# One decoder-layer step on one core: recurrent sample states in four partition quarters, and the first norm from token rows

## The chip, the cores and the metric

The kernel runs on one core of a Trainium2 chip. The time is device microseconds (us) of that core for one execution. The engines are TensorE (PE; PEld is its weight load), VectorE (DVE), ScalarE (ACT), GpSimd (POOL) and SyncE (SP), which issues nearly all transfers. Each engine runs its own instructions in the order in which they were written and waits on semaphores for the others.

## What is computed

One layer of a hybrid decoder, in float32, for a prompt of 512 tokens and a sample group of 8 sequences with 4 tokens each. All 544 tokens share the weights; the model width is 1024.

```python
x = x + 0.5 * swiglu_1(rmsnorm(x))            # 1024 -> 2816 -> 1024
z = rmsnorm(x) @ w_in                         # q,k,v of 8 attention heads; q,k,v,o and gates of 4 mLSTM heads
x = x + concat(attention, mlstm) @ w_out
x = x + 0.5 * swiglu_2(rmsnorm(x))
# mLSTM, one head, one sequence, T tokens, state C (128 x 128), n (128), m:
num = A @ v + w_inter * (q @ C)               # A: gated causal q.k within the chunk
den = rowsum(A) + w_inter * (q @ n)
h   = num / max(|den|, exp(-m_t))
C   = w_c * C + (w_s * k)^T @ v               # n likewise; w_c, w_s from the gates
```

The attention is a dilated causal window with three dilations. For the sample group it reads a cache of 2048 earlier positions per sequence. For the mLSTM each of the 8 sample sequences brings its own state of 4 heads, which is read once and written once. Prompt states start at zero.

## The kernel before

Activations lie transposed: model width on the 128 partitions, tokens along the free dimension (512 prompt columns S, then 32 sample columns). `x` is eight such tiles of 128 x 544.

**Products.** Each weight block and each activation tile is split into a high and a low half (`whi`, `wlo`; `xh`, `xl`), and three products high*high, high*low, low*high are summed in PSUM. A product covers 272 columns, so one 128-row step of one output block is six matmuls (`mm<-xh,whi` and so on, recorded at L283, where the helper `mm` stands). ScalarE makes `whi`, VectorE makes `wlo`. Two PSUM tiles `mm` take the products; four tiles `aux` serve all else: transposes (helper `tr`, L288), attention, mLSTM, norms. All calls of the other engines go through one wrapper, so all have line 224 and are told apart by their tiles.

**Stages.** Feed-forward 1 (a first plain part of four column blocks, then blocks in a fast form with seven products in place of eight, `oh`/`ol`), the input projection `w_in` with the attention and the mLSTM worked in between its products, the output projection `w_out`, feed-forward 2. The first pass of `w_out` multiplies the outputs of the first three mLSTM heads (`mixed[4..6]`, operands `mh`/`ml`), the second pass head four and the attention.

**Order.** While the program is built, a class `Order` keeps a clock for each engine from a small cost table. Everything beside the products is a generator ("thread") that says when its inputs will be ready and how many `aux` tiles it needs; between two steps of the products, `poll` lets those threads write whose time has come, by priority. What results is one fixed order for each engine. Nothing is reordered at run time.

**The start.** Transfers bring the four token blocks `xt` of the left model half, the sample rows `xst`, the first weight block, the right half, the second weight block, then the "up" weights. `start` (L821) transposes eight groups of four blocks and one of sample rows; each group is copied out, scaled into `xh` and `xl`, and squared (`sq`: six on POOL, two on ScalarE). The squares are added up (three on POOL, four on VectorE), a matmul with `onesd` sums over partitions, and the norm's factor `rb` follows in passes over 272 columns. The products take x without that factor; the rescale `zg = mm * rb` applies it.

**The mLSTM for the sample group** (`ml_k`, `ml_v`, `ml_head`, L1393 to L1610). The 32 sample tokens lie on partitions 0 to 31. Two tiles `C0`, each with four sequences' states of 128 x 129 (the last column is n), are read by one matmul for the part within the chunk (`aTs`, `vs`) and eight for the states, all adding to the same 32 rows; `qm` holds the scaled queries, masked once for each sequence. Then POOL spreads the values by sequence (`vb`) and scales the states by `w_c`; four matmuls of 32 rows (`kws`, `vb`), two sequences each, make the additions, and VectorE adds them to the states, which go out by a transfer. The head's output `hN` (prompt) and `hS` (sample) is normed, transposed, gated (`hf`) and split for `w_out`.

## Time and profile before

| | |
|---|---|
| median of 3 runs | 1160.46 us (1159.03 to 1163.38) |
| the profiled execution | 1159.89 us, its span 1158.1 us |
| busy in the span | PE 97%, PEld 92%, DVE 68%, ACT 44%, POOL 16% |
| products on TensorE | 7680, of 272 columns each |
| mean rate of transfers | 124 GB/s |

The stages by the trace: transposes and the first products to about 40 us, feed-forward 1 to about 403 us, `w_in` with attention and mLSTM to about 690 us, `w_out` to about 777 us, feed-forward 2 to the end. In a row of the timeline or of the groups, "128*32" behind a matmul is the part of the array that it uses (rows * columns), "128x129" the moving operand, "x16" the count of records, and "[2.54 <-ACT hS]" idle time before it and what ended it. Matmuls overlap, so the time that one takes from the engine is read from the start of the next.

### The profile page before, as it was taken

The page shows a single profiled execution, that of the slowest core. Times are in us where ns is not written, and L with a number is a line of the kernel's source. Part 1 is how long each engine was busy: PE and PEld are TensorE (multiplying, and loading weights), DVE is VectorE, ACT ScalarE, POOL GpSimd, SP SyncE. Part 2 cuts the span into 40 slices and gives each one's busy share as a digit, 9 for nine tenths or more (in the row PEclk, how much of TensorE's full clock was granted, in tenths as well). Part 3 has the DMA queues.
Part 4 walks back from the last instruction along what each step waited for, and adds up shares of the span by engine and source line. Part 5 has one row for each costly group of instructions (what it writes and reads, how often), then busy time and mean ns, then how long its engine had stood idle before and what let it go on. Part 6 is the DMA issues. An engine that isn't in the chain of part 4 may idle for free.

```text
span 1158.1 us, 21205 instructions
## 1 busy us (share of the span) xinstructions
PE 1127.3 (97%) x8722; PEld 1068.9 (92%) x8722; DVE 790.9 (68%) x1169; ACT 512.9 (44%) x913; POOL 189.5 (16%) x165
## 2 busy tenths in 40 slices
PE   6999999999999998999999998999999999999998
PEld 5999999999999998988977785999999999999998
DVE  5798337873586789889785455679883488627851
ACT  4455215551345456546542444354551255414541
POOL 4210000000000046487554022001100000000000
PEclk9999999999999999999999997999999999999999
DMA  7213412432134264766797641433142142422232
GB/s 220 79 38 118 138 39 74 145 111 93 35 120 134 88 208 109 214 208 190 235 311 247 210 162 30 138 110 110 35 149 74 38 143 76 146 74 74 64 102 59
DMA packets 140620, 143.20 MB, mean 124 GB/s; under 512 B 8068, under 2 KB 119204, under 8 KB 140524
## 3 DMA queue, kind: packets, MB, share of 16 engines
q1 hardware_dynamic: 140460, 141.84, 39.3%
q8 instruction: 69, 1.13, 0.4%
q14 instruction: 27, 0.22, 0.1%
q0 software_dynamic: 64, 0.00, 0.0%
HBM read 130.44 MB, written 9.15 MB: 121 GB/s over the span
## 4 chain that ended last, share of the span: by engine, by line
PE 82%; DVE 10%; ACT 3%; issue 2%; DMA 2%; SPq 0%; POOL 0%; ACTq 0%; DVEq 0%
PE mm L283 67%; PE aux L283 13%; PE aux L288 3%; DVE wlo L224 2%; ACT whi L224 1%; DMA kv<-in_cache_k_win_dram 1%; DVE rs L224 1%; DVE ws L224 1%; DVE dn L224 1%; DVE wraw L224 1%; DMA xt<-in_x_prompt_dram 0%; DVE bcum L224 0%; DVE xl L224 0%; DVE mo L224 0%; DVE cb L224 0%
## 5 line engine op out<-in xcount | busy, mean ns | idle before, releaser
L224 ACT CAST whi<-wraw 128x1024 fp32r<-128x1024 f32 (+3 forms) x180 | 173.9, 987 | 139.9 <-PE mm L283 115.4
L224 DVE TENSOR_TENSOR wlo<-wraw,whi 128x1024 fp32r<-128x1024 f32 (+3 forms) x180 | 211.7, 1185 | 19.8 <-ACT whi L224 19.6
L283 PE MATMUL mm<-oh,wlo 128*128 128x272 f32 x720 | 209.4, 291 | 2.9 <-DVE wlo L224 2.9
L283 PE MATMUL mm<-oh,whi 128*128 128x272 f32 x720 | 207.4, 288 | 0.0
L283 PE MATMUL mm<-ol,whi 128*128 128x272 f32 x720 | 207.2, 288 | 0.0
L283 PE MATMUL mm<-xh,whi 128*128 128x272 f32 x720 | 160.1, 304 | 0.8 <-DVE zg L224 0.7
L283 PE MATMUL mm<-xh,wlo 128*128 128x272 f32 x720 | 150.1, 290 | 2.9 <-DVE wlo L224 2.9
L283 PE MATMUL mm<-xl,whi 128*128 128x272 f32 x720 | 150.4, 291 | 0.0
L283 PE MATMUL mm<-hh,whi 128*128 128x272 f32 x704 | 146.2, 289 | 0.0
L283 PE MATMUL mm<-hl,whi 128*128 128x272 f32 x704 | 145.6, 288 | 0.0
L283 PE MATMUL mm<-hh,wlo 128*128 128x272 f32 x704 | 145.6, 288 | 0.0
L224 DVE SCALAR_TENSOR_TENSOR x<-mm,x 128x544 f32<-128x544 f32 x48 | 34.8, 725 | 157.9 <-PE mm L283 157.9
L283 PEld LDWEIGHTS mm<-oh,wlo 128*128 128x128 f32 x720 | 135.4, 188 | 6.0 <-DVE wlo L224 4.7
L283 PEld LDWEIGHTS mm<-ol,whi 128*128 128x128 f32 x720 | 135.6, 188 | 0.0
L283 PEld LDWEIGHTS mm<-oh,whi 128*128 128x128 f32 x720 | 135.5, 188 | 0.0
L283 PEld LDWEIGHTS mm<-xh,whi 128*128 128x128 f32 x720 | 114.1, 191 | 13.8 <-issue 10.7
L283 PEld LDWEIGHTS mm<-xh,wlo 128*128 128x128 f32 x720 | 114.4, 191 | 3.3 <-DVE wlo L224 3.3
L283 PEld LDWEIGHTS mm<-xl,whi 128*128 128x128 f32 x720 | 114.4, 191 | 0.0
L283 PEld LDWEIGHTS mm<-hl,whi 128*128 128x128 f32 x704 | 110.4, 188 | 0.0
L283 PEld LDWEIGHTS mm<-hh,whi 128*128 128x128 f32 x704 | 110.3, 188 | 0.1
L283 PEld LDWEIGHTS mm<-hh,wlo 128*128 128x128 f32 x704 | 110.4, 188 | 0.0
L224 ACT CAST whi<-ws 128x1024 fp32r<-128x1024 f32 x54 | 56.7, 1051 | 99.7 <-DVE ws L224 99.7
(295 smaller groups left out, 1930.9 us busy)
## 6 DMA issues: line engine op xcount, KB each, us to landing
wraw<-in_ffn_w_gate_dram SPq DMA_DIRECT2D x38, 512.0 KB
wraw<-in_ffn_w_up_dram SPq DMA_DIRECT2D x36, 512.0 KB
wraw<-in_ffn_w_down_dram SPq DMA_DIRECT2D x16, 1024.0 KB
kv<-in_cache_k_win_dram SPq DMA_DIRECT2D x56, 256.0 KB
kv<-in_cache_v_win_dram SPq DMA_DIRECT2D x56, 256.0 KB
wraw<-in_w_in_dram SPq DMA_DIRECT2D x16, 512.0 KB
wraw<-in_ffn_w_down_dram SPq DMA_DIRECT2D x8, 768.0 KB
wraw<-in_w_in_dram SPq DMA_DIRECT2D x6, 1024.0 KB
```

What stands on the lines that cost most here:

```text
L224: r = fn(*args, **kw)
L283: nc.tensor.matmul(out, lhsT, rhs, start=start, stop=stop, **kw)
L288: nc.tensor.transpose(out, in_, idn)
```

## The change

It has two parts.

**Sample states in four quarters.** A helper `four` issues the same matmul four times, to output partitions 0, 32, 64 and 96, in four column quarters of the array. With it the sample rows of keys and values, and of the gate columns, are transposed into all four quarters, so `kws`, `vs` and `hS` have 128 partitions. Quarter g stands for sequences 2g and 2g+1. The states are read by twelve matmuls: four for the part within the chunk, and twice four in which quarter g reads its own sequence; `qm` holds two masks in place of eight. Each state update is a matmul on the 32 rows of one quarter for two sequences (`vb` has the two sequences side by side, made by two ScalarE copies with a 0/1 column `bm4`); two such matmuls, on different rows of the array and into different `aux` tiles, are issued together, and VectorE scales and adds each state in one operation. POOL's `vb` and state scaling are gone, as is one memset. The last transpose of `hS` becomes a matmul with a constant `own` that picks each token's quarter. A column of `bm4` makes the unused rows' denominators harmless.

**First norm from token rows.** `from_rows` squares and sums the rows of `xt` and `xst` as they land (two blocks of each half on ScalarE, two and the sample rows on VectorE), makes the factor on 128 x 5 elements, spreads it with five small matmuls on diagonals, and copies it to `rb`. The tiles `sq` and their sums go for the first norm. Transposes run no more than three groups ahead of the products. The first two weight blocks are now two tiles, which fills the three raw buffers until the first is split. There is one general tile less (61 for 62).

```diff
-NT2 = 62
+NT2 = 61
...
+            if self.rows:
+                yield R(xh) - 0.3
+                dve.scalar_tensor_tensor(xl, x, g, xh.bitcast(F32), op0=OP.mult, op1=OP.subtract)
+                self.x[m] = (xh, xl)
+                return
...
+        def from_rows(self, blocks):
...
+                    if b < 2:
+                        act.activation(j[0:n], x, AF.Square, accum_out=ssa[:, b, c:c + 1])
+                    else:
+                        dve.tensor_tensor_reduce(out=j[0:n], in0=x, in1=x, scale=1.0, scalar=0.0, op0=OP.mult,
+                                                 op1=OP.add, accum_out=ssd[0:n, b - 2, c:c + 1])
...
+            yield from rsqrt(y, v, t)
+            dg, ds = t2("dg", (P, S)), t2("ds", (NS, NS))
...
+                mm(pa[:, b * P:(b + 1) * P], onesd, dg[:, b * P:(b + 1) * P])
+            mm(pb_[:, 0:NS], onesd[0:NS], ds)
...
-                products(j, ps, ks)
+                for k in ks:
+                    products(j, ps, (k,))
+                    used[0] = max(used[0], k + 1)
+                    od.poll()
...
-                yield R(xs_, *blocks), 2
+                yield R(xs_, *blocks), 2, lambda: 4 * c + m < used[0] + 3
...
+    def four(p, n, lhsT, rhs, **kw):
+        for g in range(4):
+            mm(p[NS * g:NS * g + NS, 0:n], lhsT, rhs, beside=g > 0, tile_position=(0, NS * g), **kw)
...
-            tr(p[0:NS, 0:P], k[:, S:N], ident)
-            kws = small("kws", (NS, P), 3)
+            four(p, P, k[:, S:N], ident)
+            kws = small("kws", (P, P), 3)
...
-            tr(p[0:NS, 0:P], vt[:, S:N], ident)
-            act.copy(vs[:, 0:P], p[0:NS, 0:P])
+            four(p, P, vt[:, S:N], ident)
+            act.copy(vs[:, 0:P], p[:, 0:P])
...
+            vb = small("vb", (P, 2, V1), 3)
+            for j in range(2):
+                act.activation(vb[:, j], vs, AF.Copy, scale=bm4[:, j:j + 1])
...
-        mm(o, aTs, vs, start=True, stop=False)
-        for b in range(B):
-            mm(o, qm[:, b, :], C0[b // HB][:, b % HB, :], start=False, stop=b == B - 1)
...
-            pool.tensor_tensor(vb, bc(vs, 1, HB), bc(bm32[:, i * HB:(i + 1) * HB], 2, V1), op=OP.mult)
-            pool.tensor_tensor(c0, c0, bc(wc[:, i * HB:(i + 1) * HB], 2, V1), op=OP.mult)
...
+        four(po, V1, aTs, vs[0:NS], stop=False)
+        for j in range(2):
+            for g in range(4):
+                mm(po[NS * g:NS * g + NS, 0:V1], qm[:, j], C0[g // 2][:, 2 * (g % 2) + j, :], start=False, stop=j == 1,
+                   beside=g > 0, tile_position=(0, NS * g))
...
-                mm(pk[:, 0:2 * V1], kws, vbs[i][:, b0:b0 + 2, :].rearrange("p b v -> p (b v)"))
-                cs = c0[:, b0:b0 + 2, :].rearrange("p b v -> p (b v)")
-                dve.tensor_tensor(cs, cs, pk[:, 0:2 * V1], op=OP.add)
...
+            pk = aux(), aux()
+            for e in range(2):
+                r_ = slice(2 * NS * i + NS * e, 2 * NS * i + NS * e + NS)
+                mm(pk[e][:, 0:2 * V1], kws[r_], vb[r_].rearrange("p b v -> p (b v)"), beside=e > 0,
+                   tile_position=(r_.start, 0))
+            for b in range(HB):
+                at_ = S + T * (HB * i + b) + T - 1
+                dve.scalar_tensor_tensor(c0[:, b], c0[:, b], W[:, at_:at_ + 1], pk[b // 2][:, b % 2 * V1:(b % 2 + 1) * V1],
+                                         op0=OP.mult, op1=OP.add)
...
-        tr(p[:, 0:NS], hS, ident[0:NS, 0:NS])
+        mm(p[:, 0:NS], hS, own)
```

Since the costs and the ready times differ, `Order` writes another order for the whole mixing stage. Three places follow. First TensorE at the start; in the order before, the last of the eight transpose groups and the first products:

```order
L288 MATMUL aux<-ident,xt 128x128 x4
L288 MATMUL aux<-ident,xst 128x32
L283 MATMUL mm<-xh,whi 128x272 x2
L283 MATMUL mm<-xl,whi 128x272 x2
L283 MATMUL mm<-xh,wlo 128x272 x2
```

and in the change, from the third group on:

```order
L287 MATMUL aux<-ident,xt 128x128 x4
L287 MATMUL aux<-ident,xst 128x32
L282 MATMUL mm<-xh,whi 128x272 x2
L282 MATMUL mm<-xl,whi 128x272 x2
L282 MATMUL mm<-xh,wlo 128x272 x2
L287 MATMUL aux<-ident,xt 128x128 x4
L287 MATMUL aux<-ident,xst 128x32
```

Groups four to seven now stand one by one behind the first steps of the products, the eighth behind nine steps.

Second, TensorE where the fourth mLSTM head is finished, about 702 to 716 us of the profile before (`rq`, `pS` and `pT` belong to the last attention pair, `mh` to `w_out`). Before:

```order
L288 MATMUL aux<-ident,hN 128x128 x4
L288 MATMUL aux<-ident,hS 128x32
L283 MATMUL aux<-vs,aTs 32x129
L283 MATMUL aux<-C_7917,qm 32x129 x4
L283 MATMUL aux<-C_7918,qm 32x129 x4
L283 MATMUL aux<-rq 128x512 x2
L288 MATMUL aux<-ident,pS 128x128 x4
L283 MATMUL aux<-pT,vr 64x128 x4
L283 MATMUL aux<-rq 128x384 x2
L283 MATMUL mm<-mh,whi 128x272 x2
```

and in the change:

```order
L282 MATMUL aux<-Cst,qw 128x129
L282 MATMUL aux<-vs,aTs 32x129 x4
L282 MATMUL aux<-C_8181,qm 32x129 x2
L282 MATMUL aux<-C_8182,qm 32x129 x2
L282 MATMUL aux<-C_8181,qm 32x129 x2
L282 MATMUL aux<-C_8182,qm 32x129 x2
L282 MATMUL mm<-mh,whi 128x272 x2
```

Before, 25 rows without a product lie between two products of `w_out`; now the attention's last rows stand further ahead, among the products of `w_in`, and 72 products follow this readout before the next other row.

Third, POOL in the last head. Before, from the mask of the queries to the end of the head:

```order
L224 TENSOR_TENSOR qm<-qw,ca 128x256
L224 MEMSET ss 128x5
L224 TENSOR_TENSOR hN<-hN,rs 128x512
L224 COPY nP<-Cst 128x1
L224 COPY nS<-C_7333 128x4
L224 COPY nS<-C_7334 128x4
L224 TENSOR_TENSOR vb<-vs,c_bm_111 32x516
L224 TENSOR_TENSOR C_7917<-C_7917,W 128x516
L224 TENSOR_TENSOR vb<-vs,c_bm_111 32x516
L224 TENSOR_TENSOR C_7918<-C_7918,W 128x516
L224 TENSOR_TENSOR hf<-hf,mo 128x544
```

and in the change:

```order
L223 TENSOR_TENSOR hf<-hf,mo 128x544
L223 TENSOR_TENSOR qm<-qw,ca 128x64
L223 COPY nP<-Cst 128x1
L223 TENSOR_TENSOR hN<-hN,rs 128x512
L223 COPY nS<-C_8181 128x4
L223 COPY nS<-C_8182 128x4
```

The third head's `hf` now stands ahead of the fourth head's mask, and nothing stands between the fourth head's mask and its `hN` but a copy of one column.

More of the change, by code (lines that the diff above doesn't have):

```diff
@@ L315, in __init__ @@
             self.begun = self.n = 0
+            self.rows = False
             self.rb = None
@@ L370, in __init__ @@
             self.ops = {}
+        def from_rows(self, blocks):
+            self.rows = True
+            ssa, ssd = small("ssa", (P, 2, 2)), small("ssd", (P, 3, 2))
+            v, y, t = (small(n, (P, CH + 1)) for n in ("rsv", "rsy", "rst"))
+            pool.memset(ssd, 1.0)
+            for c in range(2):
+                xb, xs_ = blocks[c]
+                for b, x in enumerate(xb + [xs_]):
+                    yield R(x) - 0.2
+                    n = NS if b == CH else P
+                    j = t2("sj", (P, 512))
+                    if b < 2:
[3 more added lines that the diff above has]
+                                                 op1=OP.add, accum_out=ssd[0:n, b - 2, c:c + 1])
+            yield R(ssa, ssd) - 0.2
+            dve.tensor_tensor(v[:, 0:2], ssa[:, :, 0], ssa[:, :, 1], op=OP.add)
+            dve.tensor_tensor(v[:, 2:5], ssd[:, :, 0], ssd[:, :, 1], op=OP.add)
+            dve.tensor_scalar(v, v, 1.0 / D, EPS, op0=OP.mult, op1=OP.add)
+            yield R(v) - 0.2
+            yield from rsqrt(y, v, t)
+            dg, ds = t2("dg", (P, S)), t2("ds", (NS, NS))
+            for b in range(CH):
+                dve.tensor_scalar(dg[:, b * P:(b + 1) * P], ident, y[:, b:b + 1], float(D), op0=OP.mult, op1=OP.mult)
+            dve.tensor_scalar(ds, ident[0:NS, 0:NS], y[0:NS, CH:CH + 1], float(D), op0=OP.mult, op1=OP.mult)
+            yield R(dg, ds) - 0.2, 2
+            pa, pb_ = aux(), aux()
+            for b in range(CH):
+                mm(pa[:, b * P:(b + 1) * P], onesd, dg[:, b * P:(b + 1) * P])
+            mm(pb_[:, 0:NS], onesd[0:NS], ds)
+            r = t2("rb")
+            copy(r[:, 0:S], pa)
+            copy(r[:, S:N], pb_[:, 0:NS])
+            done(pa, pb_)
+            self.rb = r
+            od.spawn(self.operands(), 2, R(r) - 0.2, 0, lambda: self.x[KD - 1] is not None)
         def finish(self):
@@ L780, in ffn_jobs @@
                 cols = [c0, c0 + P]
-                rg, ru = Raw(wg, 0, 8, cols), Raw(wu, 0, 8, cols)
-                jobs += [Job(rg, i, xs, gate(f + i)) for i in range(2)]
+                ru = Raw(wu, 0, 8, cols)
+                if jobs or f0 or f:
+                    rg = [Raw(wg, 0, 8, cols)] * 2
+                    jobs += [Job(rg[i], i, xs, gate(f + i)) for i in range(2)]
+                else:
+                    jobs += [Job(Raw(wg, 0, 8, [cols[i]]), 0, xs, gate(f + i)) for i in range(2)]
                 jobs += [Job(ru, i, xs, up(f + i)) for i in range(2)]
@@ L840, in start @@
                 done(pa, pb_)
-                od.spawn(n1.add(4 * c + m), 1)
+                od.spawn(n1.add(4 * c + m), 0)
         yield 0
-    od.spawn(start(), 0)
+    od.spawn(start(), 1)
+    od.spawn(n1.from_rows(xin), 2)
     rb = lambda: n2.rb
@@ L869, in hybrid_layer_kernel @@
     causS = const("causS", (NS, NS))
-    bm32 = const("bm32", (NS, B))
+    bm4 = const("bm4", (P, 3))
+    own = const("own", (P, NS))
     hmask = const("hmask", (P, NH))
@@ L1220, in gates @@
             tr(pc[:, c * 96:(c + 1) * 96], st[0:96, c * P:(c + 1) * P], ident[0:96, 0:96])
-        tr(pc2[0:NS, 0:96], st[0:96, S:N], ident[0:96, 0:96])
+        four(pc2, 96, st[0:96, S:N], ident[0:96, 0:96])
         tr(pc2[:, 128:128 + B * NM], nrow, ident[0:B * NM, 0:B * NM])
@@ L1407, in post @@
             p = aux()
-            tr(p[0:NS, 0:P], k[:, S:N], ident)
-            kws = small("kws", (NS, P), 3)
-            dve.tensor_scalar(kws, p[0:NS, 0:P], cols[0:NS, CH, 1, h:h + 1], None, op0=OP.mult)
+            four(p, P, k[:, S:N], ident)
+            kws = small("kws", (P, P), 3)
+            dve.tensor_scalar(kws, p[:, 0:P], cols[:, CH, 1, h:h + 1], None, op0=OP.mult)
             done(p)
@@ L1420, in post @@
             done(full, kind="mm")
-            vm, vs = t2("vm", (P, CH, V1)), small("vs", (NS, V1), 3)
+            vm, vs = t2("vm", (P, CH, V1)), small("vs", (P, V1), 3)
             pool.memset(vm[:, :, P:V1], 1.0)
@@ L1478, in ml_head @@
         yield R(E, W) - 0.3, 0, lambda: "kws" in d and "vs" in d
-        q, k, kw, kws, vm, vs = (d[x] for x in ("q", "k", "kw", "kws", "vm", "vs"))
+        q, k, kw, kws, vm, vs, vb = (d[x] for x in ("q", "k", "kw", "kws", "vm", "vs", "vb"))
         for c in range(CH):
```

59 lines of the change are left out of this document (22 added, 37 removed).

## The prediction

> **What bounds the kernel now.** I read the page first, then busy time by stretches, then the chain of waits in order of time, then single rows. The page:
>
> ```profile
> PE 1127.3 (97%) x8722; PEld 1068.9 (92%) x8722; DVE 790.9 (68%) x1169; ACT 512.9 (44%) x913; POOL 189.5 (16%) x165
> PE 82%; DVE 10%; ACT 3%; issue 2%; DMA 2%; SPq 0%; POOL 0%; ACTq 0%; DVEq 0%
> ```
>
> TensorE is busy 97% of the span and carries 82% of the chain that ends last. So time is won in three ways only: fewer TensorE slots, fewer TensorE waits, or the same slots at a higher clock. The stretches (span, then busy time and count of PE, PEld, DVE, ACT, POOL, then granted clock, DMA share, GB/s) show where the last two are to be had:
>
> ```profile
> 8.50:18.30 9.80, 9.80 (x37) 6.57 (x37) 5.95 (x11) 7.11 (x14) 7.85 (x7) 1.00 1.10 340
> 23.00:28.00 5.00, 5.00 (x24) 5.00 (x24) 5.00 (x6) 0.11 (x1) 0.67 (x1) 1.00 0.40 110
> 38.65:78.05 39.40, 39.40 (x314) 39.40 (x315) 36.60 (x52) 17.81 (x26) 8.85 (x5) 1.00 0.28 82
> 80.00:100.00 20.00, 18.23 (x141) 17.57 (x140) 18.94 (x23) 10.94 (x17) 0.70 (x1) 1.00 0.35 107
> 600.00:620.00 20.00, 20.00 (x150) 14.30 (x147) 11.18 (x25) 5.75 (x18) 11.60 (x12) 1.00 1.02 361
> 696.60:718.50 21.90, 18.71 (x74) 12.14 (x74) 11.24 (x36) 9.26 (x32) 6.80 (x9) 0.61 0.09 28
> ```
>
> A product of 272 columns takes 39.40/314 = 0.125 us in the steady stretch, but 5.00/24 = 0.21 us at 23 to 28 us: TensorE runs there at about half speed, although the clock column says 1.00 so early. The other slow place is 696.6 to 718.5 us, the end of the mixing stage: 3.2 us idle, and the rest at a mean clock of 0.61. The chain of the start (start, length, what):
>
> ```profile
> 8.50 7.07 PE aux L288 x26
> 20.43 2.04 DVE wlo L224
> 22.52 10.75 PE mm L283 x62
> 38.65 39.40 PE mm L283 x312
> 581.27 8.45 DMA kv<-in_cache_k_win_dram
> ```
>
> Transposes come first, then VectorE holds up the first low-half product until 22.52, and from 38.65 on TensorE leads.
>
> **The change, term by term: the start.** It removes nine POOL operations, four VectorE additions and the 544-column norm; it adds squares of token rows. Rows with the costs (the fourth is one of TensorE's waits: for whom, us, times, longest):
>
> ```profile
> 9.17 1.11 PE L288 MATMUL aux<-ident,xt 128*128 128x128 f32 x4
> 16.31 4.12 DVE L224 SCALAR_TENSOR_TENSOR xl<-x,gcol,xh 128x544 fp32r<-128x544 f32 x3
> 24.68 0.77 DVE L224 SCALAR_TENSOR_TENSOR xl<-x,gcol,xh 128x544 fp32r<-128x544 f32 x1
> PE mm L283 <- DVE zg L224: 0.7, 1, 0.7
> L224 DVE CUSTOM_DVE_ANT_0 pS<-aux,ca 128x512 f32<-128x512 f32 x8 | 5.2, 680 | 3.8 <-PE aux L283 3.8
> ```
>
> Three xl took 4.12 us beside POOL's squares, where one alone takes 0.77, so about 1.8 us of VectorE time is contention that goes. A row square on VectorE is nearest to the 680 ns row: six of them are 4.1 us. Removed are four additions as wide as the 0.77 us row (3.1 us) and six half-width passes of the old norm. So VectorE's total stays about the same, but it begins earlier. I walk its new order from the landing of the last of the first blocks (8.5 us, where the transposes of the chain set in): two row squares 1.4 (a first ran before), copies 1.8 at about the same rate, 0.4 of waiting for the second group, an xl 0.8, a square 0.7, the first wlo 1.0 (the chain has 2.04 us for two). That is 6.1, so 14.6 us instead of 22.5. Yet five of the eight transpose groups are then still to come, each 1.11 us and a small one, say 1.28 us: 6.4 us. So TensorE is ahead by 22.5 - 14.6 - 6.4 = 1.5 us. The rescale zg no longer waits for the norm (0.7 us of TensorE's waiting), which makes 2.2 us. VectorE, nearly full from 38 to 90 us, is some 6 us ahead, so I let the 1.8 us of waits at 80 to 100 go too: **4.0 us**. Upper end: at full clock from the start, some 30 products would save 0.085 us each and five groups 0.75 us each (0.36 us for four transposes further down), 6.3 us, of which VectorE's walk, whose last xl ends near 27 us, leaves about 5: 9.0. Lower end: 2.2.
>
> The row 8.50:18.30 decides between the ends: TensorE was busy all 9.8 us with transposes, and the products after it still took 0.21 us. Amid transposes the clock will hardly rise sooner. (The Trainium skill, "TensorE: Matmul & The Clock Gate", Part 4 on the PE-mode transpose, says transposes do not count as busy for the clock; this row agrees. By the rule the term is 4.0; if transposes counted it would be 9.0.)
>
> **The recurrent sample part.** Rows (start, length, engine, operation, count; the next start gives the slot). A plain fp32 matmul leaves two records, a transpose one:
>
> ```profile
> 576.33 1.11 PE L283 MATMUL aux<-kt,qd 128*32 128x132 f32 x32
> 577.36 1.09 PE L283 MATMUL aux<-pT,vr 128*64 128x128 f32 x16
> 580.53 0.92 PE L283 MATMUL aux<-rq 64*128 64x384 f32 x4
> 581.38 0.44 PE L288 MATMUL aux<-ident,vt 128*128 128x128 f32 x2
> 605.78 0.40 PE L283 MATMUL aux<-vs,aTs 32*32 32x129 f32 x2
> 606.11 1.96 PE L283 MATMUL aux<-C,qm 128*32 128x129 f32 x16
> 608.00 0.52 PE L283 MATMUL mm<-xh,whi 128*128 128x272 f32 x2
> 608.86 0.60 PE L288 MATMUL aux<-ident,mk 128*128 128x128 f32 x4
> 609.22 0.50 PE L283 MATMUL mm<-xh,whi 128*128 128x272 f32 x2
> 623.08 0.70 PE L283 MATMUL aux<-vb,kws 32*128 32x258 f32 x2
> 623.71 0.52 PE L283 MATMUL mm<-xh,whi 128*128 128x272 f32 x2
> 704.07 0.63 PE L283 MATMUL aux<-vs,aTs 32*32 32x129 f32 x2 [0.54 <-ACT hf L224]
> 708.07 1.13 PE L283 MATMUL aux<-rq 64*128 64x512 f32 x4
> ```
>
> Readout: nine matmuls one after another take 608.00 - 605.78 = 2.22 us. Now there are three groups of four beside each other. The sixteen of kt,qd, in column quarters of nearly this size, take 1.03 us, 0.26 a group. Three groups and a change-over make 0.85, so 1.37 saved in three heads; in the last, at half clock, 708.07 - 704.07 = 4.0 falls to 0.85: **7.3 us**. Unpacked, twelve at 1.89/8 = 0.236 would be 2.8 us, a loss of 0.6 a head.
>
> State update: a lone matmul of 258 columns costs 0.63 us; sixteen become eight pairs on different row quarters. Row pairs overlap in rq: two of 384 columns in 0.85 us, where 129 columns at 0.236 would make 1.40. At 0.63 a pair the term is **5.0 us**; without overlap, 0. I take the overlap, though 32-row pairs are not in this trace.
>
> Added: nine transposes of the sample rows become four matmuls each, 0.09 (0.36/4) to 0.26: **-1.5 us**; not overlapped, 0.94 each, -7.7. The last transpose of each head becomes a full-height product, about 0.15 more: **-0.6 us**.
>
> VectorE and POOL, by form:
>
> ```profile
> L224 DVE SCALAR_TENSOR_TENSOR Cst<-Cst,W,aux 128x129 f32<-128x129 f32 x12 | 4.2, 348 | 1.2 <-PE aux L283 0.8
> L224 DVE TENSOR_TENSOR C<-C,aux 128x258 f32<-128x258 f32 x16 | 6.7, 417 | 5.7 <-PE aux L283 5.7
> L224 DVE TENSOR_TENSOR dn<-dn,cols 32x1 f32<-32x1 f32 x4 | 7.9, 1984 | 0.1
> L224 POOL TENSOR_TENSOR vb<-vs,c_bm 32x516 f32<-32x516 f32 x8 | 9.8, 1222 | 0.0
> L224 POOL TENSOR_TENSOR C<-C,W 128x516 f32<-128x516 f32 x8 | 8.4, 1045 | 8.9 <-issue 7.1 <-PE aux L283 1.8
> ```
>
> Eight scaled additions of 0.348 replace four of 0.417: +1.1 us on VectorE a head. POOL loses 18.2 us; with it goes the 1.98 us that a one-column dn takes while POOL works, which alone pays for the additions. Two small ScalarE copies a head hide under TensorE, as ScalarE is 44% busy. These cost nothing on the path; uncovered, they would be 4.4 us.
>
> **The end of the mixing stage.** There the last head's chain runs bare:
>
> ```profile
> 708.53 2.51 DVE L224 TENSOR_TENSOR dn<-dn,cols 32x1 f32<-32x1 f32 x1
> 708.70 1.04 POOL L224 TENSOR_TENSOR C<-C,W 128x516 f32<-128x516 f32 x1
> 709.71 1.32 POOL L224 TENSOR_TENSOR hf<-hf,mo 128x544 f32<-128x544 f32 x1
> 711.74 1.12 PE L288 MATMUL aux<-ident,pS 128*128 128x128 f32 x4 [2.54 <-ACT hS L224]
> ```
>
> POOL's scaling holds dn, dn holds hS on ScalarE, and behind hS waits the copy for the attention's transposes; hf of the third head stands in POOL's queue behind the same scaling, and w_out's first products need it. In the new order the last attention pair is finished among the input products, and products stand between the head's steps. So I expect the stretch 696.6:718.5 at full clock and unbroken: 18.71 us x 0.61 = 11.4, a gain of 7.3, less 2.5 already counted in readout and updates, and 3.2 idle: **8.0 us**. Ends: 0, if the gap moves, and 8.0.
>
> Against it I set one new wait as large as the idle time of this stretch, since the whole order of the stage is new: **-3.2 us**, ends 0 and -6.4 (two of them). FFN products are unchanged in number.
>
> **Sum:** 4.0 + 7.3 + 5.0 - 1.5 - 0.6 + 8.0 - 3.2 = 19.0. Against the profiled execution, 1159.89 us (span 1158.1; 1.8 lie around it), that is 1140.9; the runs' median, 1160.46, lies 0.6 higher. I say 1141.
>
> **The rivals.**
>
> A. The end stays slow: the narrow matmuls keep the clock down, or the gap moves to another wait. For it: from 696.6 to 708 TensorE was nearly always busy and yet slow. Against: the new order puts full products between. 19.0 - 8.0 = 11.0 gained: 1149.
>
> B. The cache transfers pace the sample attention. For it: the 8.45 us of the chain at 581 and a DMA share of 1.02 at 600:620. Against: transfers also waited for state updates that now come sooner. What is won earlier (start 4.0, the first head's 1.37 and 1.25) is lost there, 6.6: 1148.
>
> C. The clock rises early at the start: 5 more, 1136. Against it stands the row 8.50:18.30.
>
> D. Slower: the packed matmuls do not overlap. Readouts lose 2.4, transposes 7.7, the last products 0.6, updates win 0, the end wins nothing, as the added work fills it, one new wait costs 3.2; only the start's 4.0 stays, so 9.9 are lost: 1170. With updates and end lost too, it decides once a group of four costs 0.55 us (the remaining 6.0 us over 21 groups, above 0.26). Against: 0.26 in kt,qd.
>
> E. Each change of the array's split empties TensorE: for the length of a narrow matmul's latency, about 0.27 us, where the slots above already hold 0.09. Some 26 new changes at 0.18 are 4.7 us: 1146. Against: kt,qd hands over to pT,vr, another split, with no gap beyond its 1.03 us. (The Trainium skill, "TensorEngine Tiling (Array Packing)", Key Properties, says that changing the tiling mode drains TensorE; no row here shows the longer price.)
>
> **The numbers.** Forecast 0.46, A 0.18, B 0.12, C 0.12, D 0.05, E 0.05, rest 0.02. The forecast's own range is 1134 to 1147. With the upper ends, start 5 more and no new wait, the time is 1133; the runs spread by some 2 us around their median, so 1131. A, B and E end by 1150, and a second wait adds 3.2. Range 1131 to 1153, which leaves out D and the far tails. Half a per cent, 5.8 us, is about what a measurement here can tell from no change: faster 0.86, same 0.08 (A or B with a second wait), slower 0.06 (D and the rest).
>
> **What would show it.** First low-half product near 15 us, and the unbroken run of products beginning near 36; otherwise the start is wrong. Readout records of a head within 0.9 us, update pairs at 0.63 us; pairs at 1.1 or groups at 0.9 mean D. Clock near 1.00 at w_out's first products, with no stretch of 20 us at 0.6; if there is one, A. TensorE waiting for cache tiles before kv,pTA means B. The forecast fails most simply by a new VectorE wait in the mixing stage larger than 3.2 us.

## The result, and the profile after

The changed kernel takes 1141.47 us (median of 4 runs, 1140.47 to 1142.33), the kernel before 1159.74 us beside it. The ratio is 0.984, with a 95% interval of 0.9812 to 0.9868. The profiled execution took 1140.47 us, its span is 1138.7 us, 19.4 us shorter than before. First the page of the changed kernel, with the same two lines as before:

```profile
PE 1110.7 (98%) x8819; PEld 1057.8 (93%) x8819; DVE 783.9 (69%) x1199; ACT 516.1 (45%) x926; POOL 155.5 (14%) x137
PE 79%; DVE 11%; DMA 3%; ACT 3%; issue 3%; POOL 1%; SPq 1%; ACTq 0%; DVEq 0%; POOLq 0%
```

TensorE was busy 1127.3 us and is now busy 1110.7: 16.6 us are busy time, 2.8 are waits. Where they went shows in the stretches (columns as in the prediction):

```profile
60.00:80.00 20.00, 18.15 (x141) 17.50 (x140) 17.49 (x22) 9.15 (x14) 3.88 (x2) 1.00 0.09 20
80.00:100.00 20.00, 19.46 (x153) 19.02 (x152) 17.58 (x22) 10.95 (x15) 0.00 (x0) 1.00 0.35 107
440.00:460.00 20.00, 16.59 (x105) 15.74 (x105) 19.80 (x17) 11.13 (x23) 16.60 (x12) 0.83 0.42 115
500.00:520.00 20.00, 18.25 (x172) 16.41 (x169) 19.59 (x38) 10.65 (x28) 14.83 (x13) 1.00 0.62 188
540.00:560.00 20.00, 17.82 (x140) 15.42 (x137) 18.60 (x28) 11.86 (x32) 14.31 (x11) 1.00 0.74 244
600.00:620.00 20.00, 20.00 (x173) 13.95 (x172) 13.82 (x28) 8.51 (x16) 9.25 (x6) 1.00 0.96 337
700.00:720.00 20.00, 20.00 (x174) 18.51 (x173) 15.40 (x44) 9.89 (x31) 1.43 (x3) 1.00 0.44 129
```

At 700 to 720 us, where TensorE had been busy 16.89 us at a clock of 0.63, it is busy throughout at 1.00. At 500 to 520 and 540 to 560 us it now idles 3.9 us, where the kernel before had 0.9. The chain at the start (start, length, what):

```profile
13.49 1.15 DVE wlo L223
...
14.69 0.82 PE mm L282 x2
...
18.26 1.09 PE aux L287 x5
19.36 1.66 PE mm L282 x6
...
21.70 0.94 PE mm L282 x6
22.64 0.61 PE aux L287 x5
...
29.25 35.67 PE mm L282 x282
...
74.20 2.26 DVE ws L223
...
86.64 12.04 PE mm L282 x94
```

The first low-half product comes at 14.69 us (22.52 before). Six products take 1.66 us up to 21.02 and 0.94 us behind it, a transpose group 1.09 and then 0.61: the clock has risen at about 21 us, amid transposes. The first product behind the 96 of the first two blocks, by the timeline, begins 3.9 us sooner than before (34.71 against 38.65 us). But the run that began at 89.61 begins at 86.64, so only 3.0 us are left there; VectorE, which leads the chain from 66 to 86 us, took the rest.

The readout and an update pair of the first head:

```profile
512.48 0.42 PE L282 MATMUL aux<-vs,aTs 32*32 32x129 f32 x8
512.83 0.65 PE L282 MATMUL aux<-C,qm 128*32 128x129 f32 x16
513.41 0.52 PE L282 MATMUL mm<-xh,whi 128*128 128x272 f32 x2
...
527.20 0.70 PE L282 MATMUL aux<-vb,kws 32*128 32x258 f32 x4
527.83 0.52 PE L282 MATMUL mm<-xh,whi 128*128 128x272 f32 x2
```

A readout takes 513.41 - 512.48 = 0.93 us, a pair 0.63.

The table divides the stage from the sums of the second norm (`aux<-sq,onesd`, near 405 us) to those of the last, in us. "Slots" are the times from the start of each record to the start of the next, idle time taken off; "small transposes" are all of `mk`, `mv` and `st`. The other kernels are those of the experiments.

| kernel | stage | idle | readouts | updates | small transposes | other aux | products |
|---|---|---|---|---|---|---|---|
| before | 368.8 | 10.0 | 10.7 | 10.8 | 4.3 | 95.4 | 237.5 |
| changed | 352.3 | 8.3 | 3.7 | 5.1 | 7.8 | 88.9 | 238.6 |
| changed again | 351.1 | 6.6 | 3.7 | 5.1 | 7.8 | 88.2 | 239.7 |
| start only | 361.3 | 9.5 | 8.9 | 10.0 | 4.3 | 90.8 | 237.8 |
| quarters only | 351.3 | 8.3 | 3.7 | 5.1 | 7.8 | 88.2 | 238.3 |
| POOL relief only | 369.9 | 14.4 | 8.9 | 10.1 | 4.7 | 89.7 | 242.2 |
| changed, rotary on VectorE | 342.8 | 5.3 | 3.6 | 5.1 | 7.4 | 85.3 | 236.0 |
| before, rotary on VectorE | 355.8 | 5.8 | 8.7 | 10.1 | 5.0 | 88.4 | 237.8 |

Before it the changed kernel is 3.0 us ahead (the stage begins at 404.3, not 407.3 us), behind it both need 382 us.

### The profile page after: what moved, and what is told of

It is laid out like the page before. It is cut to its first block, busy times and chain, and to the rows that moved or that the text cites. A ratio compares the mean times of both kernels' runs of the same rounds, so it can differ in the third digit from the quotient of the medians.

```text
span 1138.7 us, 21430 instructions
## 1 busy us (share of the span) xinstructions
PE 1110.7 (98%) x8819; PEld 1057.8 (93%) x8819; DVE 783.9 (69%) x1199; ACT 516.1 (45%) x926; POOL 155.5 (14%) x137
## 4 chain that ended last, share of the span: by engine, by line
PE 79%; DVE 11%; DMA 3%; ACT 3%; issue 3%; POOL 1%; SPq 1%; ACTq 0%; DVEq 0%; POOLq 0%
PE mm L282 65%; PE aux L282 11%; DVE wlo L223 3%; PE aux L287 3%; ACT whi L223 2%; DMA kv<-in_cache_k_win_dram 2%; DVE ws L223 2%; DVE rs L223 1%; DVE wraw L223 1%; SPq L223 1%; DMA xt<-in_x_prompt_dram 1%; DVE cb L223 1%; DMA wraw<-in_ffn_w_up_dram 1%; DVE mo L223 0%; DVE bcum L223 0%
## 5 line engine op out<-in xcount | busy, mean ns | idle before, releaser
L223 DVE TENSOR_TENSOR wlo<-wraw,whi 128x1024 fp32r<-128x1024 f32 (+3 forms) x180 | 209.0, 1170 | 20.8 <-ACT whi L223 20.3
L282 PEld LDWEIGHTS mm<-xh,whi 128*128 128x128 f32 x720 | 113.8, 191 | 12.8 <-issue 10.7
```

The source lines that it names most:

```text
L223: r = fn(*args, **kw)
L282: nc.tensor.matmul(out, lhsT, rhs, start=start, stop=stop, **kw)
```

## The experiments

My theory after the first look: the start gives 3 us and the quarters 16, of which the shorter readouts and updates are certain; the closed end of the stage comes from the new order. Rivals: the gain is the start's in a roundabout way, the packed matmuls are short for another reason than the quarters, the end is POOL's doing, narrow work keeps the clock down. All ratios are to runs of the kernel before on the same chip.

### The two parts alone

Start only: the new `Norm`, `from_rows`, `run` and `start`, the old mLSTM. Quarters only: the reverse.

> The kernel before with the new start alone (first norm from token rows, transposes amid products, two raw tiles); mLSTM as before. Theory: the two parts add up, and the start is worth what the changed kernel shows at the first steady run and keeps to the end of feed-forward 1: the run of products that began at 89.61 us begins near 86.6, so about -3.0 us, a time near 1156.7 (ratio 0.9974). The clock rises near 21 us, amid the transposes. Rival 1 (the lead is lost in the mixing stage, whose waits end by transfers or by VectorE and not by TensorE): within 1 us of before. Rival 2 (my term of 4.0 holds once the mixing stage is the old one): 1155.7 or less.

> The changed kernel with the old start (norm by squares of columns, all eight transpose groups ahead of the products). Theory: the mLSTM part is worth 16.4 us by itself, as the changed kernel's mixing stage is 16.4 us shorter: near 1143.3 (ratio 0.986). Rival (the full clock at the end of the mixing stage came from the way the work happened to fall after an earlier start): only the slots go, 6.9 us of readout and 5.7 of updates less 3.4 of four-fold transposes, 9 us, near 1150.5, and a stretch at a clock near 0.6 is there again before the products of the output projection.

Measured: start only 1153.85 us, ratio 0.9966 (0.9943 to 0.9989); quarters only 1143.32 us, 0.9884 (0.9849 to 0.9920). Their product is 0.985, the whole change 0.984, so the parts add up. In its profile the start-only kernel reaches the mixing stage only 0.5 us ahead of before: the second half of the tokens landed at 13.3 us where the changed kernel had it at 12.8, and the clock fell behind a wait near 80 us. The mixing stage of this kernel, whose mLSTM is that of before, is 7.5 us shorter than in the profile of before, although TensorE's 2729 records of the stage stand in the same order in both. At the end of the stage its row reads

```profile
700.00:720.00 20.00, 17.53 (x125) 12.36 (x125) 12.43 (x37) 11.90 (x36) 6.37 (x8) 1.00 0.20 60
```

2.5 us idle as before, but at a clock of 1.00. The half clock at that place is not a fixed property of that mLSTM, nor of its order. The 54 runs of the kernel before that stand beside these experiments say the same: they reach from 1149.1 to 1163.2 us, their mean granted clock from 1.000 to 0.984, and the two go together (correlation -0.85, 8 us for 0.01 of the clock).

### What makes the packed matmuls short

Readout, the same twelve matmuls in another order:

```diff
-        four(po, V1, aTs, vs[0:NS], stop=False)
-        for j in range(2):
-            for g in range(4):
-                mm(po[...], qm[:, j], ...)
+        for g in range(4):
+            mm(po[...], aTs, vs[0:NS], stop=False, beside=g > 0, tile_position=(0, NS * g))
+            for j in range(2):
+                mm(po[...], qm[:, j], ...)
```

> The changed kernel with the twelve matmuls of each readout in another order: all three of a quarter one after another, then the next quarter. Same matmuls, same place among the products. Theory (four neighbours in four column quarters run beside each other, and matmuls of one quarter follow one another): a readout goes from 0.93 us to 2.2 to 2.8 us, so +5 to +7.5 us in four heads, near 1147. Rival (a narrow matmul is cheap wherever it lies, and the readout became short since there are other operands and no run of nine sums in one place): 0.93 stays, no change, 1141.

Update, both matmuls of a pair on the same rows:

```diff
-                r_ = slice(2 * NS * i + NS * e, 2 * NS * i + NS * e + NS)
+                r_ = slice(2 * NS * i, 2 * NS * i + NS)
```

> The changed kernel with both matmuls of each state update taken from the same 32 rows of the array (the first's operands twice, so half of the sample states are updated with the wrong sequences' values; count, shapes and order stay). Theory (the pair is cheap because it lies on different row quarters): a pair goes from 0.63 us to about 1.2, in eight pairs +4.5 us, near 1146. Rival (the second matmul of a pair is hidden in the first's latency anyway): 0.63 to 0.75 a pair, at most +1 us.

Readout by quarter: 1147.35 us, ratio 0.9919 (0.9888 to 0.9950). One quarter after another takes

```profile
512.58 0.40 PE L282 MATMUL aux<-vs,aTs 32*32 32x129 f32 x2
512.91 0.63 PE L282 MATMUL aux<-C,qm 128*32 128x129 f32 x4
...
516.15 0.52 PE L282 MATMUL mm<-xh,whi 128*128 128x272 f32 x2
```

3.57 us for 0.93, 0.30 a matmul, more than the 2.2 to 2.8 expected; the quarters do not overlap even where one ends and the next begins. So four neighbours in four column quarters cost 0.31 us, and four in one quarter 1.19. Four readouts cost 10.6 us more of TensorE, and the ratio is 0.008, about 9 us, above that of the whole change.

Pairs on the same rows: the pair

```profile
526.56 1.13 PE L282 MATMUL aux<-vb,kws 32*128 32x258 f32 x4
527.62 0.52 PE L282 MATMUL mm<-xh,whi 128*128 128x272 f32 x2
```

takes 1.06 us, not 0.63, eight pairs 3.4 us. So the second matmul of a pair is free only on other rows. The time of the whole, 1142.31 us, 0.9875 (0.9843 to 0.9906), lies 0.0035 above the changed kernel's, which agrees with 3.4 us but is no more than the intervals hold.

### Who closes the end of the stage

The changed kernel once more, for comparison, and two kernels that set POOL and order against each other. POOL relief only, on the kernel before:

```diff
-            pool.tensor_tensor(vb, bc(vs, 1, HB), bc(bm32[...], 2, V1), op=OP.mult)
-            pool.tensor_tensor(c0, c0, bc(wc[...], 2, V1), op=OP.mult)
+            dve.tensor_tensor(vb, bc(vs, 1, HB), bc(bm32[...], 2, V1), op=OP.mult)
...
-                dve.tensor_tensor(cs, cs, pk[:, 0:2 * V1], op=OP.add)
+                for b in range(b0, b0 + 2):
+                    dve.scalar_tensor_tensor(c0[:, b], c0[:, b], W[:, at_:at_ + 1], pk[...], op0=OP.mult, op1=OP.add)
```

POOL load back, on the changed kernel, hidden from `Order`:

```diff
+        nc.gpsimd.tensor_copy(qm[:, :, 0:1], qm[:, :, 0:1])
+        for _ in range(4):
+            nc.gpsimd.tensor_tensor(load[0:NS], load[0:NS], epsc[0:NS].broadcast_to((NS, 2 * V1)), op=OP.mult)
+            nc.gpsimd.tensor_tensor(load, load, epsc.broadcast_to((P, 2 * V1)), op=OP.mult)
```

> The changed kernel once more, to stand beside the other runs of this group. Expected: 1141.5 within 1.5 us, and a spread of its executions of about 5 us, less than that of the kernel before (14 us in the group of runs ahead of this one).

> The kernel before, its start, its 32-row readouts and its 32-row state updates, with one thing changed: POOL's spreading of the values and scaling of the states goes to VectorE (the scaling in the addition, as in the changed kernel). TensorE's instructions are the same in number and shape. The order comes out with the last attention pair ahead and w_out's products behind the last readout, as in the changed kernel. Theory (the end of the mixing stage was a matter of POOL's work in the last head and of the order that it brought): the stretch of 3.2 us idle and a clock of 0.61 is gone, the stage is 368.8 - 8 = 361 us long, the time near 1151 (ratio 0.993), and the spread is small. Rival (fewer TensorE slots closed the end): the gap stays, no change within 2 us.

> The changed kernel with its order kept, and POOL work put back behind each readout: four operations of 32x258 and four of 128x258 on a scratch tile, whose results nobody uses, about as long as the old spreading and scaling (4.5 us a head), begun when the readout has been done. Theory (it is the order of TensorE's work that keeps the end closed; products stand behind each step of the last head): within 2 us of the changed kernel. Rival (POOL's load itself holds hN and hS back): the transposes of hN in the last head come 4 to 5 us later, TensorE waits for them, and with one fall of the clock it is 1146 to 1150.

Measured: changed again 1140.60 us, 0.9844 (0.9826 to 0.9861); POOL load back 1141.38 us, 0.9854 (0.9838 to 0.9871); POOL relief only 1159.96 us, 1.0026 (1.0007 to 1.0045).

In the changed order POOL's work costs nothing that shows. Here POOL is busy where it was idle, and TensorE does not notice:

```profile
700.00:720.00 20.00, 20.00 (x173) 18.51 (x173) 16.63 (x44) 9.82 (x30) 8.06 (x12) 1.00 0.42 129
```

POOL relief alone closed the same stretch, and yet my expectation of 1151 failed. Its rows at the end and in the middle of the stage:

```profile
600.00:620.00 20.00, 15.46 (x101) 12.63 (x100) 12.90 (x28) 5.62 (x17) 7.07 (x6) 0.83 0.85 274
700.00:720.00 20.00, 20.00 (x172) 18.31 (x171) 13.83 (x40) 8.57 (x19) 3.09 (x6) 1.00 0.51 168
```

and its timeline at the largest gap:

```profile
605.11 1.26 POOL L224 TENSOR_TENSOR pr<-kv,qb 128x512 f32<-128x512 f32 x1 [9.70 <-DMA kv<-in_cache_k_win_dram]
605.22 0.69 DVE L224 TENSOR_TENSOR ml<-aux,mh 128x512 fp32r<-128x512 f32 x1 [9.95 <-DMA out_dram<-ks]
605.97 1.23 PE L283 MATMUL aux<-vm,aT 128*128 128x129 f32 x4 [4.35 <-DVE ml L224]
```

POOL waited 9.7 us for a cache tile and VectorE 10 us for a transfer out, and TensorE stood 4.35 us behind VectorE, with the clock down behind it. The end was won and the middle lost: idle time in the stage rose from 10.0 to 14.4 us. So the order closes the end, with POOL's work there or not; but each new order of this stage has waits of its own, and closing one place is no net gain by itself.

### Is the gain bound to this order?

The other order is made by giving POOL's two-input operations of the rotary tiles and of the plain blocks' hidden product to VectorE, once on the changed kernel and once on the kernel before:

```diff
-                    pool.tensor_tensor(z, zg[f], z, op=OP.mult)
+                    dve.tensor_tensor(z, zg[f], z, op=OP.mult)
...
-            pool.tensor_tensor(z2, z, tabs[i][0], op=OP.mult)
-            pool.tensor_tensor(r, r, tabs[i][1], op=OP.mult)
-            pool.tensor_tensor(z2, z2, r, op=OP.add)
+            dve.tensor_tensor(z2, z, tabs[i][0], op=OP.mult)
+            dve.tensor_tensor(r, r, tabs[i][1], op=OP.mult)
+            dve.tensor_tensor(z2, z2, r, op=OP.add)
```

> The changed kernel with two more groups of POOL's two-input operations given to VectorE: the three multiplications and additions of each rotary tile (440 to 520 us, where one VectorE operation beside them takes 3.69 us in place of 0.69) and the hidden product zu of the plain blocks (each costs the VectorE operation beside it about 1.1 us). Theory (POOL's and VectorE's two-input operations hold each other up, so moving them is cheaper than leaving them): the 3.4 us wait for rs near 445 us goes, and with it, in the executions where the clock falls, about 2.8 us more; the start's lead of 4.2 us keeps the 1.2 us that it lost near 66 to 86 us; in feed-forward 2 the 1.8 us wait near 810 us shrinks. Together 4 to 8 us, near 1135. Rival (VectorE, at 18.7 to 19.8 of 20 us there, cannot take 24 operations of 0.72 us): the waits grow, 1145.

> The kernel before with the same two groups of operations (the rotary tiles' and zu) given to VectorE, and nothing of the change. The question is whether the change's 17 us of this chip hold on another order of the stage. If all of it is TensorE work taken out and waits closed for good, this kernel lies 17 to 19 us above the changed kernel with the same edit (1132.3): near 1150. If only the taken-out work is lasting (readout 6.9, updates 5.7, less 3.4 for four-fold transposes, and 3 at the start: 12 us) and the rest was a lucky order, near 1144. If it stays at 1157, the edit works only together with the change.

Measured: on the changed kernel 1132.27 us, 0.9769 (0.9749 to 0.9789), 8 us less than the changed kernel on the same chip; on the kernel before 1147.20 us, 0.9910 (0.9878 to 0.9942). The wait near 445 us is gone. VectorE in the changed kernel:

```profile
440.59 3.69 DVE L223 TENSOR_TENSOR rs<-rs,rv 128x544 f32<-128x544 f32 x1
...
445.83 1.73 DVE L223 TENSOR_TENSOR ry<-ry,rs 128x544 f32<-128x544 f32 x1
```

and with the rotary work on its own queue:

```profile
439.95 0.72 DVE L223 TENSOR_TENSOR rs<-rs,rv 128x544 f32<-128x544 f32 x1
...
441.18 0.72 DVE L223 TENSOR_TENSOR ry<-ry,rs 128x544 f32<-128x544 f32 x1
```

The two take 5.42 us beside POOL's work and 1.44 without it, while a rotary operation costs VectorE about 0.7 us when it does it itself. (The Trainium skill, "SBUF — State Buffer", section "SBUF: two separate sides", says that a VectorE operation with two SBUF inputs and a GpSimd operation lock each other out for a whole instruction; these rows agree.)

The new order of the stage is part of the 8 us, so not all of it is shown to be POOL's doing.

The kernel before with this edit also bears on the end of the stage. Its readouts and updates are the unpacked ones and POOL still spreads and scales in the last head, but products stand between the head's steps, and the end is nearly closed, with 1.05 us idle at a clock of 1.00:

```profile
700.00:720.00 20.00, 18.95 (x148) 16.90 (x147) 16.88 (x47) 9.15 (x28) 5.55 (x7) 1.00 0.22 70
```

On this other order the change is worth 14.9 us by the medians (1147.20 to 1132.27, from two groups of runs; 16 by the ratios) where it was worth 17 on the old one (1157.76 to 1140.60; 18 by the ratios). The intervals of the ratios, 2 to 4 us to each side, do not tell the two apart. The kernel before with this edit lies midway between the first two cases that I had set. With nearly equal idle time (5.8 and 5.3 us) the two stages differ by 13.0 us: 5.1 in readouts, 5.0 in updates, 2.4 lost in small transposes, and the remaining 5.3 in the half clock behind a wait near 590 us of the slower kernel and in smaller items. So about 7 us in the stage are slots that are gone at full clock (7.7 here, 6.6 between the start-only and the quarters-only kernel), and 3 to 5 us come from the start. The rest of the 17, 5 to 7 us, is waits and half clock. Some of it is there in both comparisons; whether every order would show it stays open.

### Narrow work, transposes and waits, and the clock

The changed kernel with extra stretches between the down-projection blocks of feed-forward 2:

```diff
+            if kind == "rows":
+                for _ in range(40):
+                    mm(p[0:NS, 0:P], ident[:, 0:NS], ident)
+            elif kind == "corner":
+                for _ in range(40):
+                    mm(p[0:NS, 0:P], ident[0:NS, 0:NS], ident[0:NS, :])
...
+            elif kind == "turn":
+                for _ in range(100):
+                    tr(p[:, 0:P], ident, ident)
+            else:
+                for _ in range(kind):
+                    mm(p[:, 0:NS], ident, ident[:, 0:NS])
+                    act.copy(s, p[:, 0:NS])
+                    mm(p[:, 0:NS], ident, s)
```

> The changed kernel with six idle-purpose stretches written between the down-projection blocks of feed-forward 2, whose results nobody uses: 40 matmuls on 128 rows and 32 columns of the array, one after another; 100 transposes; 40 matmuls on 32 rows and 32 columns; 40 matmuls on the whole array; then one round trip TensorE-ScalarE-TensorE, and further on three in a row. Theory (the clock at the end of the mixing stage fell because of TensorE's short waits, not because of narrow work): the first, third and fourth stretch run at the rate seen elsewhere (0.236, about 0.17 and 0.236 us each) and the products behind them keep 0.125 us; the three round trips let the clock fall and the products behind them take 0.22 us for about 6 us; one round trip does it in some executions. Rival A (narrow work keeps the clock down): behind the first or third stretch, or within it, the spacing doubles. For the transposes I expect the clock to fall within the stretch or behind it, as the 9.8 us of transposes at the start never raised it.

Clock and times by stretches (the first: 128 rows by 32 columns; then the transposes and the products behind them; then 32 by 32 in two parts):

```profile
858.84:867.69 8.85, 8.85 (x82) 8.65 (x81) 1.86 (x2) 0.96 (x1) 0.00 (x0) 1.00 0.05 16
891.90:902.73 10.83, 10.83 (x102) 10.83 (x101) 0.72 (x1) 0.00 (x0) 0.00 (x0) 1.00 0.04 13
902.73:910.00 7.27, 7.27 (x61) 7.27 (x60) 0.96 (x2) 0.00 (x0) 0.00 (x0) 1.00 0.01 2
1012.70:1017.00 4.30, 4.30 (x41) 4.14 (x41) 1.86 (x2) 0.96 (x1) 0.00 (x0) 1.00 0.09 30
1017.00:1025.19 8.19, 8.19 (x43) 6.29 (x40) 0.00 (x0) 0.00 (x0) 0.00 (x0) 0.54 0.01 2
```

and the three round trips in the timeline, with the products behind them:

```profile
1162.33 0.41 PE L282 MATMUL aux<-probe,ident 128*128 128x32 f32 x2 [0.28 <-ACT probe L223]
...
1163.29 0.41 PE L282 MATMUL aux<-probe,ident 128*128 128x32 f32 x2 [0.33 <-ACT probe L223]
...
1164.25 0.48 PE L282 MATMUL aux<-probe,ident 128*128 128x32 f32 x2 [0.33 <-ACT probe L223]
...
1165.50 0.80 PE L282 MATMUL mm<-hh,whi 128*128 128x272 f32 x2
```

Matmuls that use 32 columns and all rows, whole matmuls (also at 1.00) and, against my expectation, 10.8 us of transposes leave a full clock as it is. A round trip with one wait of 0.28 us did so too. Three round trips, with waits of 0.28, 0.33 and 0.33 us within 2.2 us, brought it down: the first two products behind them take 0.80 us where such a row has 0.50 to 0.52 at full clock. But their matmuls move only 32 columns each, so TensorE also had little to do between the waits, and the probe does not tell the two apart. Matmuls of 32 rows by 32 columns brought the clock down without any wait, about 5 us after they began: their records start 0.109 us apart, then 0.213. That is the sign which the expectation had given to rival A for this stretch; my theory had products at 0.125 us behind it.

In the kernel before, the 32-by-32 matmuls take 0.33 us of a readout, so they alone did not do it. Two waits stand where its slow stretch begins:

```profile
695.84 0.30 PE L288 MATMUL aux<-ident,pS 128*128 128x128 f32 x1 [0.24 <-ACT ms L224]
696.68 0.67 PE L283 MATMUL aux<-vb,kws 32*128 32x258 f32 x2 [0.54 <-DVE sden L224]
```

They are not enough to explain it. The start-only kernel has the same matmuls in the same order with the same two waits, and its clock stays at 1.00:

```profile
695.48 0.30 PE L287 MATMUL aux<-ident,pS 128*128 128x128 f32 x1 [0.24 <-ACT ms L223]
696.32 0.67 PE L282 MATMUL aux<-vb,kws 32*128 32x258 f32 x2 [0.54 <-DVE sden L223]
```

Nor does a longer wait always bring a fall: the changed kernel waits 1.75 us before 519.59 at a clock of 1.00. And once the clock was down in the kernel before, waits did not hold it there: from 697.6 to 707.8 us TensorE was busy for 9.66 of 10.2 us at a mean clock of 0.50, among transposes, matmuls on a part of the array and some on all of it. So rival A's "the narrow matmuls keep the clock down" is neither shown nor refuted. The same instructions with the same waits met a fall in one execution and none in another, and what decides it stays open. (The Trainium skill, "TensorE: Matmul & The Clock Gate", "Why this matters for your kernels", warns of idle gaps above about 3 us; the falls at 697 us and in the probe came without one.) The probe has no stretch of 32 rows by 128 columns, the form of `vb,kws`, which stands four times between 692.9 and 700.4 us of the kernel before.

### Transposes first

```diff
-                yield R(xs_, *blocks), 2, lambda: 4 * c + m < used[0] + 3
+                yield R(xs_, *blocks), 2
...
+        od.need(lambda: xT[KD - 1] is not None)
         first = [(j, slot()) for j in jobs[:2]]
```

> The changed kernel with all eight transpose groups ahead of the first product, as before; the norm from token rows stays. Theory (interleaving is worth the 6.4 us of transposes that stand behind the first products, in part, and the early products raise the clock): the first low-half product comes near 20 us in place of 14.7, and as transposes alone do not raise the clock, it rises about 6 us after the products begin, near 26 us and not 21; the 96 products of the first two blocks end 3 to 4 us later. The steady run behind the wait near 80 us gets 1 to 3 us of it: 1142 to 1144. Rival (what wins at the start is VectorE's work alone): no change within 1 us.

Measured: 1138.23 us, 0.9816 (0.9795 to 0.9838). The expectation failed: it is not slower than the changed kernel (0.9844 on this chip), perhaps faster by 0.3%, which the intervals do not settle.

```profile
18.47 0.82 PE L282 MATMUL mm<-xh,whi 128*128 128x272 f32 x2
...
22.71 0.65 PE L282 MATMUL mm<-xh,whi 128*128 128x272 f32 x2
...
23.86 0.41 PE L282 MATMUL mm<-xh,whi 128*128 128x272 f32 x2
```

The clock rises about 5 us after the first product, near 23.4 us, though 10 us of transposes ran before it. Yet the products lose nothing: no transpose stands among them any more, and the steady run behind the last wait begins at 85.07 us, not 86.64. So the interleaving is not needed; what wins at the start is the rest of the change there, by the chain VectorE's earlier work.

### Both edits together

The rotary tiles and `zu` on VectorE, and all transposes first.

> The changed kernel with the rotary tiles and zu on VectorE and with all transposes ahead of the products: the two edits that did best, together. Theory (the start's gain is VectorE's earlier work and does not need the interleaving; the two edits touch different places): the ratio to the kernel before is 0.977 (rotary tiles) less what transposes first brought, 0 to 0.003: 0.974 to 0.977, near 1129 to 1132. If the start's lead is lost in feed-forward 1 or the new order of the mixing stage draws other waits: up to 0.982, 1138.

Measured: 1132.07 us, 0.9796 (0.9768 to 0.9823), no better than the rotary edit alone (1132.27 us, 0.9769). The ratio lies outside the 0.974 to 0.977 that I expected and within the case set beside it, a lost lead or other waits of the new order. In the profiles the lead is kept (the stage begins at 402.6 us, with the rotary edit alone at 402.2), but the stage takes 346.9 us against 342.8. Part of that is chance, since the profiled execution of the rotary edit was its fastest. These two are the fastest of this study, about 25 us below the kernel before.

## Why the prediction was right, point by point

1141 was predicted and 1141.47 measured. The terms, against the two profiles (stage table, us gained; the last term is what is left of the spans' difference when the others are taken off):

| term | predicted | measured |
|---|---|---|
| start | +4.0 | +3.0 |
| readouts | +7.3 | +6.9 |
| state updates | +5.0 | +5.7 |
| four-fold transposes | -1.5 | -3.4 |
| last product of each head | -0.6 | +0.3 |
| end of the stage, less one new wait | +4.8 | +6.9 |
| sum | 19.0 | 19.4 |

That the sum came so close is partly luck: start and transposes fell short by 2.9 us together, and the last two terms made up 3.0. It is luck also that the profiled execution of the kernel before was a typical one, as the paragraph on the end shows.

**The start** came out for another reason than I gave. VectorE's walk was right to 0.1 us (14.6 predicted, 14.69 measured), though it began at 7.75 us and not at 8.5 and then waited 0.64 us for the second half of the tokens, which the walk did not have. Wrong was "amid transposes the clock will hardly rise sooner": it rose at 21 us, 6.3 us after the first low-half product and amid transposes, rival C's event. The row of pure transposes that I went by, and the rule beside it (the Trainium skill, "TensorE: Matmul & The Clock Gate", Part 4), hold where the clock is down (again in the transposes-first run, 10 us without a rise), not where products stand between; and at a full clock 10.8 us of transposes did not lower it. The unbroken run began at 29.25, not near 36. It brought 1 us less and not 5 more, since the step "I let the 1.8 us of waits at 80 to 100 go too" failed: with products faster, VectorE is what they wait for from 66 to 86 us, 2.4 us in all. And the 6.4 us of remaining transposes, which I subtracted, did not decide: put in front, they cost nothing more.

**Readouts and updates** stood on the row of kt,qd and on rq, and the quarters do what those rows said: 0.31 us a group of four (0.26 plus change-over predicted), 0.63 us a pair. The two runs that took the packing away showed 3.57 and 1.06 us. Rival D is out. Of rival E, the price of a change of the array's split, a part is there: a readout with its change-overs is 0.93 us against 0.85, and more of it shows in the next term. Of the 12.6 us in the two profiles, 2.7 are matmuls of the last head that ran at half clock before.

**Four-fold transposes** is the term that I mis-sized by more than two. I had taken 0.26 from kt,qd for the four and 0.09 for the one they replace. The timeline of the changed kernel has

```profile
486.32 0.60 PE L287 MATMUL aux<-ident,mv 128*128 128x128 f32 x4
486.85 0.42 PE L282 MATMUL aux<-ident,mv 128*32 128x128 f32 x8
487.21 0.52 PE L282 MATMUL mm<-xh,whi 128*128 128x272 f32 x2
```

0.36 us for the four, and 0.53 for the full transposes ahead of them, where four full ones and the small one together took 0.46 (489.23 to 489.69 us before). So the ordinary matmuls cost 0.10 more than I took, and the change from whole to quarter columns, which I left out, seems to lie in those 0.53: 0.38 a place in the mean (3.4/9), not 0.17.

**The end of the stage** went as forecast: clock 1.00, unbroken, the idle time there gone; and waits opened elsewhere, as the new-wait term said, 4 us at 500 to 560 where there had been 1.35. Over the whole stage idle time fell by 1.7 us, and the slots of work that is the same in both kernels by about 5.2, for the most part the half clock of the old end. But I took that half clock for a property of the place. The start-only profile, with the same order, does not have it (1.00), so the term is worth 8 us only against executions like the one profiled. Of the 54 runs of the kernel before, 40 have a mean granted clock of 0.992 or less, where the profiled one has 0.990, so most lose about as much to half clock as it did; at which places is not on record.

**My reason for the end**, POOL's scaling holding dn, hN and hf, may hold for the old order, but it does not decide. With POOL's work put back the new order stays closed, and on the other order the kernel before is nearly closed with POOL's work in place. With POOL's work taken away alone the end closes too, but in another order, and the middle opens, for no gain. B's mechanism, cache transfers that pace the stage, did not hold the changed kernel up at 600 to 620 us (20.00 busy), but waits for transfers stand in the gap of the POOL-relief kernel: POOL's for a cache tile, and VectorE's, behind which TensorE stood, for a transfer out.

## What to carry to other kernels

Small matmuls that are written next to each other on different column or row quarters cost about what one of them costs; written so that neighbours share a quarter, they cost their sum. Where a planner fixes the order, an edit moves waits all over the stage: compare the slots of the work that the edit touches apart from idle time and clock, and test the edit on a second order before its gain is called its own. Look for an operation of VectorE that takes several times its usual length beside GpSimd: moving GpSimd's operations onto VectorE was worth 8 us on the changed kernel and 12 on the kernel before, the new order included.

## What the runs showed of the hardware

The same wait, 3.41 us for `rs` near 445 us, was followed by a mean clock of 0.83 at 440 to 460 us in the profile of the changed kernel, 0.91 in that of before, and by

```profile
440.00:460.00 20.00, 16.63 (x126) 16.05 (x125) 19.66 (x30) 11.63 (x23) 12.87 (x9) 1.00 0.35 86
```

a clock of 1.00 in the quarters-only kernel. So one wait costs its own 3.4 us, or about 3 us more by the half clock behind it, from one profile to the next (three kernels, one profile each). Much of the 14 us by which the 54 runs of the kernel before differ goes with the granted clock, as above. The changed kernel's two groups of four runs spread over 1.9 and 3.4 us; part of that is their small number.
